# Padding tiles move the large SBUF tiles of a two-layer backbone to multiples of 512 bytes

## The chip, the cores and the metric

The kernel runs on one core of a Trainium2 chip. The metric is the device time of one execution in microseconds (us), as the median of several runs. The engines are named as the profile names them: PE is TensorE's stream of matmuls and PEld its weight loads, DVE is VectorE, ACT ScalarE, POOL GpSimd, and SP the queue from which most transfers are issued. A matmul multiplies a stationary operand, which a weight load brings into the array first, with a moving operand, whose columns then stream through.

## The reference

The reference is a two-layer diffusion backbone on 1024 latent tokens with 256 context tokens in front of them, 1024 features wide, in float32.

```
for i in range(DEPTH):                       # DEPTH = 2
    sh1, sc1, g1, sh2, sc2, g2 = modulation(c, w_mod[i], b_mod[i])
    h = x * (1.0 + sc1) + sh1
    if i % 2 == 0:  y = retention_gla_mixer(h, ...) @ ev_w_out[j]     # 4 retention + 4 gated heads
    else:           y = window_attention(q, k, v, k_c, v_c, sink) @ od_w_out[j]
    x = sublayer_residual(x, y, g1, ln_g[i, 0], ln_b[i, 0])           # LayerNorm(alpha * x + gate * y)
    x = sublayer_residual(x, sq_relu_mlp(x * (1.0 + sc2) + sh2, mlp_w1[i], mlp_w2[i]), g2, ...)
```

The context tokens go through layer 0 as well and serve layer 1 as keys and values. The MLP is 4096 wide with a squared ReLU.

## The kernel before

All 1280 tokens are kept with features on partitions, in three chunks of 256, 512 and 512 tokens. Each float32 operand of a large product is split into two parts, `hi` and `lo` (tiles in float32r), and each product is three matmuls: hi x hi, hi x lo, lo x hi (`mm3`, L196 to L199). Weights come in by units of 128x1024: `wsplit` (L180 to L187) loads `raw`, ScalarE copies it to the `hi` half of a tile `w`, and GpSimd (or VectorE) subtracts for the `lo` half. Each tile `w` has 8 KB in every partition.

The stages in order of time are: the modulation vectors and layer 0's projections (`first_proj`, `unit_loop`, to about 180 us); the values and the reverse pass (L483 to L602, to 360 us), where the activations `xh`, `xl` are the stationary operand and the weights `wvh`, `wvl` move (L540 to L542); the forward pass with gates, output projection and residual (to 725 us); layer 0's MLP (`mlp`, L956, to 1730 us); layer 1's queries, keys and values (L1171 to L1226, to 1900 us), where again the activations `hh`, `hl` are stationary and the weights `w` move (L1201 to L1203); windowed attention with its output projection (to about 2420 us); layer 1's MLP. In the MLPs and projections of L197 to L199 the weights `w` are stationary and the activations (`hh`, `hl`, `uh`, `ul`, `yh`, `yl`) move, with 512 or 256 columns.

No planner sets the order: it is the order in which the code issues work, and each engine runs its own queue with waits on semaphores. What the change touches is memory alone. The pools are stacked in SBUF from both ends of a partition: a pool with `side="right"` grows down from the upper end, the others grow up from the lower end. `cp` (L47), the first pool on the left, holds small constants; above it lie the raw weights and the activations. On the right lie the weight tiles `w` (`w_b1`, L219, later `wg`, L483), layer 0's residual stream `acc` (`acp0`, L697) and then the keys (`kvp`, L1172). The built program gives these starts within a partition, in bytes modulo 512:

| tiles | before | after |
|---|---|---|
| weights `w` (all stages), `acc` of layer 0 | 480 | 0 |
| activations `hh`, `hl`, `uh`, `ul`, `yh`, `yl`, `xh`, `xl` | 448 | 0 |
| weights `wvh`, `wvl` of the values' stage | 448 | 0 |
| landing buffers of the weights (`rawp`) | 448 | 0 |
| first modulation weights and x in `b1` (`raw` of L230, `xs`), `lwh`, `lwl` | 0 | 64 |
| keys `kall` | 32 | 64 |
| `cs`, `ident` | 192 | 256 |

Of the kernel before, what the change touches and what calls it, by code (L numbers as in the profile page):

```python
# [19 lines left out]
P = 128  # L20
# [14 lines left out]
def backbone(ctx: ExitStack, tc: tile.TileContext, xT, cin, wmod, bmod, lng, lnb, w1, w2,  # L35
# [10 lines left out]

    cp = ctx.enter_context(pool(name="cp", bufs=1))  # L47
    rawp = ctx.enter_context(pool(name="rawp", bufs=3))
    es_p = ExitStack()
# [8 lines left out]
    def ring(*ids):  # L58
        """PSUM banks taken in turn."""
        state = [0]  # L60

        def take():
            i = ids[state[0] % len(ids)]
            state[0] += 1
            return psum.tile([P, 512], F32, tag=f"k{i}", name=nm(f"k{i}"), bufs=1)
        return take

    pM = ring(7)

# [1 line left out]
    def const(shape, name, dt=F32, pool_=None):  # L71
# [21 lines left out]

# [1 line left out]
    mod = const([2, 6, 8, 2], "mod")  # L95
# [3 lines left out]
    def mod_steps(l, s, mdp, nb=1, w=1024, tags=("raw",), bank=None):  # L99
        """Generator: one weight load and its products per step; the vectors at the end."""  # L100
        pM_ = bank or pM
# [31 lines left out]
    def mod_chunks(l, s, bank):  # L133
        """As mod_steps, 512 outputs at a time; yields the index of the chunk that a step belongs to."""
        for q in range(4):
            pt = bank()
            for k in range(0, KT, 2):
                raw = rawp.tile([P, 1024], F32, tag="raw", name=nm("raw"))
                SY.dma_start(raw.rearrange("p (a c) -> p a c", a=2),
                             wmod[l, k * P:(k + 2) * P, s * 2048 + q * 512:s * 2048 + q * 512 + 512]  # L140
                             .rearrange("(a p) c -> p a c", p=P))
                yield q
                for a in range(2):
                    for g in range(4):
                        TE.matmul(pt[32 * g:32 * g + 32, 0:P], lhsT=cs[:, k + a, :],
                                  rhs=raw[:, a * 512 + g * P:a * 512 + g * P + P], start=(k + a == 0),
                                  stop=(k + a == KT - 1))
            mt = cp.tile([P, P], F32, tag="mt", name=nm("mt"))
            S.copy(mt, pt[:, 0:P])
            TE.transpose(pt[:, P:2 * P], mt, ident)  # L150
            idx = 2 * s + q // 2
            ks = slice(4 * (q % 2), 4 * (q % 2) + 4)
            V.tensor_tensor(mod[:, l, idx, ks, :], pt[:, P:2 * P].rearrange("p (g i) -> p g i", g=4)[:, :, 0:2],
                            bm[:, l, idx, ks, None].to_broadcast([P, 4, 2]), ALU.add)
            if idx in (1, 4):
                V.tensor_scalar(osc[:, l, idx // 3, ks], mod[:, l, idx, ks], 1.0, None, op0=ALU.add)
            if idx in (2, 5):
                V.tensor_scalar(gta[:, l, idx // 3, ks], mod[:, l, idx, ks], 1.0 / ALPHA, None, op0=ALU.mult)
            yield q
# [13 lines left out]
    def reserve(pool, tags):  # L173
        """Fix the order of a pool's tags in memory."""
        for tag, shape, dt, nb in tags:
            for _ in range(nb):
                pool.tile([P] + shape, dt, tag=tag, name=nm(tag), bufs=nb)

# [1 line left out]
    def wsplit(pool, src, eng=None):  # L180
# [26 lines left out]

# [1 line left out]
    def dram(name, shape):  # L209
# [14 lines left out]
    def first_load(q):  # L224
        """Weights of the shifts and scales of feature tiles 2 q, 2 q + 1; two tiles of the sum per buffer."""
        raws = []
# [30 lines left out]
    SY.dma_start(bm, bmod.rearrange("p (l s k) -> p l s k", l=2, s=6))  # L257
# [1 line left out]
    th = const([16], "th")  # L259
# [39 lines left out]

    # ================= layer 0: projections (feature-major) =================  # L300
    def make_h(src, l, idx, j, hh, hl, tp, tag, nb=1, hi_eng=None):
# [3 lines left out]
    def h_steps(src, l, idx, j, hh, hl, tp, tag, nb=1, hi_eng=None, los=(V, G)):  # L305
        """h = src * (1 + scale) + shift, as an exact (hi, lo) pair; all (P, 8, n)."""
        n = src.shape[2]
# [11 lines left out]
    with es_b1:  # L319
# [37 lines left out]

        # lgm columns: 0-7 (d, h) on all rows; 8-11 (d, pair) in pair rows; 12-15 h in (f|b) rows
        S.activation(dret, lgm[:, 12:16], AF.Exp, scale=128.0)
# [9 lines left out]

        # low-rank gates  # L370
        gk = b1.tile([32, 4, P], F32, tag="gk", name="gk")
# [109 lines left out]

    # ================= values and reverse pass =================
    wg = ctx.enter_context(pool(name="wg", bufs=5, side="right"))  # L483
# [126 lines left out]
    def layer_norm_steps(acc, l, s, tp, ts, tq, nb, pe_sums, pL, qn=1024, tail=None):  # L610
        """acc (P, 8, n) <- LayerNorm over the features, in place."""
        n = acc.shape[2]
# [3 lines left out]
        def part(pp, src, g0, g1):  # L616
            """column groups g0..g1 of pp: sums over features of tiles 2 g, 2 g + 1 of src."""
            for kk in range(2):
# [4 lines left out]
        def mean(pp, i):  # L623
            """PSUM tile with the mean over all features on every partition."""
            pm = pL()
# [54 lines left out]
    def w_out_steps(y, wsrc, wp, acc, l, j, pW, engs=(None, None), wnext=None):  # L680
        """acc (P, 8, n) += gate / alpha * (y @ W)"""
        n = acc.shape[2]
# [10 lines left out]

    # ================= forward pass, output projection, first residual =================
    accs, hs = {}, {}
# [12 lines left out]
    with pool(name="b3", bufs=1) as b3:  # L708
# [6 lines left out]
        def load_acc(ci, o0, after):  # L715
            """A part of the residual stream, once a tile has been written."""
            G.tensor_copy(accs[ci][:, 0, o0:o0 + 1], after)
# [31 lines left out]
        def gproj(p_, g_, ln):  # L749
            """silu of the gate projections of a pair of tiles"""  # L750
            ci = chunk_of(2 * p_)
# [56 lines left out]
        for tp_ in range(NT // 2):  # L808
# [20 lines left out]
            for t in (2 * tp_, 2 * tp_ + 1):  # L829
# [30 lines left out]
                Sprev = St  # L860
                # scores (s on partitions)
                Pr = b3.tile([P, 4, P], F32, tag="Pr", name=nm("Pr"), bufs=1)
# [91 lines left out]

    # ================= MLP =================
    def mlp(l, chunks, hs, accs, wp, mp, post, fill=iter(()), tick=lambda k: None, ticks=None, early=None):  # L956
# [74 lines left out]
    class Early:  # L1031
        """Work for the first block of an MLP, in two streams that are advanced between its steps."""

# [17 lines left out]
    def new_h(hp, ci, l, mp, os_=(0, 256), los=(V, G)):  # L1051
        """Streams' parts for h of a chunk."""
        if ci not in hs:
# [51 lines left out]

    # ================= layer 1: queries, keys, values =================
    qTd = [[dr.tile([2, 2, 64, 4, P], F32, tag=f"qT{n}_{i}", name=f"qT{n}_{i}") for i in range(2)] for n in range(8)]
# [25 lines left out]
    def rotate(dst, src, nh, n):  # L1133
        """dst = src rotated; head layout (u1 32 | u2 32); src in PSUM."""
        rp = p1.tile([P, 2, 64], F32, tag="rp", name=nm("rp"), bufs=2)
# [9 lines left out]
    def transposed(kr, nj, name):  # L1145
        """kr (P, 128 nj) -> (P, 2, nj, 128): its blocks transposed, as an exact (hi, lo) pair."""
        pk = pE()
# [19 lines left out]
    for grp in range(3):  # L1167
        wu = []
        if grp == 1:
            es_a.close()  # L1170
            kvp = ctx.enter_context(ExitStack())  # L1171
            kp = kvp.enter_context(pool(name="kvp", bufs=1, side="right"))  # L1172
            kall = kp.tile([P, 2, 4, T], F32R, tag="kall", name="kall")
            wmask = const([2, P], "wmask", BF16, kp)
# [55 lines left out]

    # ================= layer 1: windowed attention, output projection, residual =================
    acp = ctx.enter_context(pool(name="acp1", bufs=1))
    hy = ctx.enter_context(pool(name="hy", bufs=1))
    yall = [hy.tile([P, KT, 512], F32R, tag=f"y{i}", name=f"y{i}") for i in "hl"]
    with pool(name="p2", bufs=1) as p2:
# [31 lines left out]
        def group(n, g):  # L1267
            """Steps of one block of queries and one group of heads: scores of four heads, then the keys' tiles."""
            blks = [b_ for b_ in (n - 1, n, n + 1) if 0 <= b_ < 8]
# [119 lines left out]

    # ================= layer 1: MLP, output =================  # L1390
    kvp.close()
# [27 lines left out]

# [1 line left out]
def _fm(w):  # L1421
    """(1024, 128 u) -> (u, 128, 8 * 128): per unit of 128 output columns."""
    u = w.shape[1] // P
# [3 lines left out]
def _col(v):  # L1427
    """(..., 1024) -> (128, ... * 8), features on partitions."""
    v = v.reshape(-1, KT, P)
# [3 lines left out]
def layout(x, c, ctx, c_ctx, w_mod, b_mod, ln_g, ln_b, mlp_w1, mlp_w2, ev_w_in, ev_ret_theta, ev_gla_gk_w,  # L1433
# [3 lines left out]
    d = {}  # L1437
# [29 lines left out]
    wqkv = od_w_qkv[0]  # L1467
    # head columns in the order (pair member, axis, frequency)
    wr = wqkv[:, :1280].reshape(1024, 20, 2, 2, 16).transpose(0, 1, 3, 2, 4).reshape(1024, 1280)
# [4 lines left out]
    d["wo1"] = _fm(od_w_out[0])  # L1474
    # constants of the shapes
    s = np.arange(P)[:, None]
# [43 lines left out]
```

## Time and profile before

| | us |
|---|---|
| median of 3 runs | 3056.57 |
| lowest and highest run | 3055.7, 3057.76 |
| span of the profiled execution | 3055.1 |

The profiled execution's own time is not listed beside the runs; its span, from the first instruction to the last, is 1.5 us shorter than the median.

A row of the page or of the trace gives the engine, the operation, output and inputs by the program's names with the shape, how often it occurs, its busy time and the mean duration. Durations of matmuls are modelled at their end, and consecutive ones overlap in the record: a matmul of 512 columns is recorded with about 0.40 us while the next one starts 0.23 us after it. What one costs in a dense stream is therefore read from starts, in the timeline.

### The profile page before, as it was taken

The page shows a single profiled execution, that of the slowest core. Times are in us where ns is not written, and L with a number is a line of the kernel's source. Part 1 is how long each engine was busy: PE and PEld are TensorE (multiplying, and loading weights), DVE is VectorE, ACT ScalarE, POOL GpSimd, SP SyncE. Part 2 cuts the span into 40 slices and gives each one's busy share as a digit, 9 for nine tenths or more (in the row PEclk, how much of TensorE's full clock was granted, in tenths as well). Part 3 has the DMA queues.
Part 4 walks back from the last instruction along what each step waited for, and adds up shares of the span by engine and source line. Part 5 has one row for each costly group of instructions (what it writes and reads, how often), then busy time and mean ns, then how long its engine had stood idle before and what let it go on. Part 6 is the DMA issues. An engine that isn't in the chain of part 4 may idle for free. (4 is left out here: it accounts for less than half of the span.)

```text
span 3055.1 us, 43318 instructions
## 1 busy us (share of the span) xinstructions
PE 2950.5 (97%) x17856; PEld 2376.8 (78%) x17856; DVE 1520.5 (50%) x2489; ACT 975.6 (32%) x1617; POOL 811.2 (27%) x609
## 2 busy tenths in 40 slices
PE   7989998999999999999999999999999999999997
PEld 4766788888878787778888777677678888888886
DVE  3654478777433333333334554666775333433336
ACT  4433344444211111111111532556653112112113
POOL 3120145544211111111110432244343122122111
PEclk9999999999999999999999999999999999999999
DMA  7367685663222222221100276122221111111011
GB/s 251 102 224 241 184 262 193 200 200 114 80 73 70 69 80 69 73 69 45 42 32 11 75 205 185 50 79 87 63 90 43 48 56 49 35 56 55 30 40 56
DMA packets 164261, 304.52 MB, mean 100 GB/s; under 512 B 13504, under 2 KB 90560, under 8 KB 163552
## 3 DMA queue, kind: packets, MB, share of 16 engines
q1 hardware_dynamic: 145648, 272.91, 28.0%
q0 software_dynamic: 6480, 16.26, 2.0%
q10 hardware_dynamic: 11936, 12.59, 1.5%
q8 instruction: 140, 2.29, 0.3%
q14 instruction: 57, 0.47, 0.0%
HBM read 257.67 MB, written 44.04 MB: 99 GB/s over the span
## 5 line engine op out<-in xcount | busy, mean ns | idle before, releaser
L186 POOL TENSOR_TENSOR w<-raw,w 128x1024 fp32r<-128x1024 f32 x210 | 508.3, 2428 | 1711.8 <-ACT w L185 1671.0
L996 DVE SCALAR_TENSOR_TENSOR acc<-k,gta,acc 128x512 f32<-128x512 f32 (+1 forms) x704 | 444.3, 649 | 861.9 <-PE k L199 855.2
L197 PE MATMUL k<-hh,w 128*128 128x256 f32 (+1 forms) x1632 | 559.5, 343 | 5.2 <-DVE hh L193 3.4
L198 PE MATMUL k<-hl,w 128*128 128x256 f32 (+1 forms) x1632 | 558.0, 342 | 4.1 <-POOL hl L194 3.5
L199 PE MATMUL k<-hh,w 128*128 128x256 f32 (+1 forms) x1632 | 554.0, 340 | 0.2 <-POOL w L186 0.2
L185 ACT CAST w<-raw 128x1024 fp32r<-128x1024 f32 x260 | 269.1, 1046 | 839.8 <-PE k L199 544.6
L197 PE MATMUL k<-uh,w 128*128 128x512 f32 (+1 forms) x1408 | 506.5, 360 | 4.0 <-DVE acc L996 3.9
L198 PE MATMUL k<-ul,w 128*128 128x512 f32 (+1 forms) x1408 | 499.6, 355 | 0.0
L199 PE MATMUL k<-uh,w 128*128 128x512 f32 (+1 forms) x1408 | 498.7, 354 | 0.0
L197 PEld LDWEIGHTS k<-hh,w 128*128 128x128 f32 x1632 | 309.7, 190 | 59.4 <-issue 16.3
L198 PEld LDWEIGHTS k<-hl,w 128*128 128x128 f32 x1632 | 309.8, 190 | 49.7 <-issue 7.4
L199 PEld LDWEIGHTS k<-hh,w 128*128 128x128 f32 x1632 | 310.0, 190 | 39.0 <-issue 2.8
L197 PEld LDWEIGHTS k<-uh,w 128*128 128x128 f32 x1408 | 264.7, 188 | 60.5 <-issue 13.6
L978 ACT ACTIVATE r<-k 128x512 f32<-128x512 f32 (+1 forms) x176 | 91.0, 517 | 665.7 <-PE k L199 664.8
L199 PEld LDWEIGHTS k<-uh,w 128*128 128x128 f32 x1408 | 264.9, 188 | 41.8 <-issue 1.0
L198 PEld LDWEIGHTS k<-ul,w 128*128 128x128 f32 x1408 | 264.8, 188 | 40.4 <-issue 0.8
L197 PE MATMUL k<-yh,w 128*128 128x256 f32 (+1 forms) x544 | 184.3, 339 | 10.3 <-DVE acc L690 10.3
L198 PE MATMUL k<-yl,w 128*128 128x256 f32 (+1 forms) x544 | 181.5, 334 | 0.0
L199 PE MATMUL k<-yh,w 128*128 128x256 f32 (+1 forms) x544 | 181.1, 333 | 0.0
L981 DVE TENSOR_TENSOR r<-r 128x1024 f32<-128x1024 f32 (+1 forms) x88 | 114.1, 1297 | 125.6 <-ACT uh L980 125.4
L670 POOL TENSOR_SCALAR acc<-acc,lg_t,lb_t 128x256 f32<-128x256 f32 x124 | 103.3, 845 | 115.6 <-DVE acc L664 46.6
L1306 DVE TENSOR_REDUCE sm<-pS 128x1 f32<-128x640 f32 (+1 forms) x128 | 100.9, 788 | 46.4 <-PE pS L1304 44.6
(300 smaller groups left out, 4415.7 us busy)
## 6 DMA issues: line engine op xcount, KB each, us to landing
raw<-in_w SPq DMA_DIRECT2D x128, 512.0 KB, 3.4
raw<-in_wo SPq DMA_DIRECT2D x72, 512.0 KB, 3.5
raw<-in_wmod SPq DMA_DIRECT2D x128, 256.0 KB, 2.7
raw<-in_wfm SPq DMA_DIRECT2D x48, 512.0 KB, 5.7
raw<-in_wmod SPq DMA_DIRECT2D x32, 512.0 KB, 4.3
kt<-kd SPq DMA_DIRECT2D x20, 512.0 KB, 5.6
qt<-qT POOLq DMA_DIRECT2D x32, 256.0 KB, 4.3
qT<-qT ACTq DMA_DIRECT2D x30, 256.0 KB, 3.7
```

Of the source, the lines that this page charges most:

```text
L185: S.copy(hi, raw)
L186: (eng or G).tensor_tensor(lo, raw, hi.bitcast(F32), ALU.subtract)
L197: TE.matmul(pt, lhsT=wh, rhs=xh, start=start, stop=False)
L198: TE.matmul(pt, lhsT=wh, rhs=xl, start=False, stop=False)
L199: TE.matmul(pt, lhsT=wl, rhs=xh, start=False, stop=stop)
L670: G.tensor_scalar(acc[:, k, :], acc[:, k, :], lg_t[:, l, s, k:k + 1], lb_t[:, l, s, k:k + 1], op0=ALU.mult, op1=ALU.add)
L978: S.activation(rf[:, i, :n], pts[i][:, :n], AF.Relu)
L981: V.tensor_tensor(rf[:, :, :n], rf[:, :, :n], rf[:, :, :n], ALU.mult)
L996: V.scalar_tensor_tensor(a_, pt[:, :n], gta[:, l, 1, m, cj(ci):cj(ci) + 1], a_, op0=ALU.mult, op1=ALU.add)
L1306: V.tensor_reduce(sm_[:, 0, i:i + 1], sall, AX.X, ALU.max)
```

## The change

Three tiles are allocated that no instruction writes or reads: 64 bytes in each partition at the beginning of `cp`, 480 bytes at the upper end of SBUF in a new pool `edge`, and 64 bytes at the beginning of `kvp`. Comments and docstrings go as well; they aren't shown.

```
     cp = ctx.enter_context(pool(name="cp", bufs=1))
+    cp.tile([P, 16], F32, tag="pad", name="pad")
+    edge = ctx.enter_context(pool(name="edge", bufs=1, side="right"))
+    edge.tile([P, 120], F32, tag="edge", name="edge")
     rawp = ctx.enter_context(pool(name="rawp", bufs=3))
...
             kp = kvp.enter_context(pool(name="kvp", bufs=1, side="right"))
+            kp.tile([P, 16], F32, tag="pad", name="kpad")
             kall = kp.tile([P, 2, 4, T], F32R, tag="kall", name="kall")
```

On PE, DVE, ACT and SP the built programs hold the same instructions with the same waits in the same order. On POOL one wait moves. It stands at the beginning of the forward pass, where `load_acc` (L715 to L718) writes one column of an `acc` tile before that tile is loaded: left and right stacks come to lie 544 bytes nearer to each other, and so a part of `acc` that had to wait for the end of an older transfer is another one. On POOL, before:

```order
L786 COPY dcm<-g_2854 128x1 [waits Activation_49]
L717 COPY acc_371_2831<-g_2854 128x1 [waits DMAHW2_49,DMAHW7_49,DMAHW0_49,Pool_49]
L836 COPY S_3190<-g_2854 128x1
L845 COPY kt_3198<-g_2854 128x1
L186 TENSOR_TENSOR w_3007<-raw_3005,w_3007 128x1024 [waits PE_49,Activation_49]
L763 TENSOR_SCALAR g_2854<-g_2854,ng 128x256 [waits DMASW1_49,DMASW0_49,Activation_49]
L717 COPY acc_371_2831<-g_2854 128x1 [waits Pool_49]
```

On POOL at the same place, after the change (three lines have been added above, so L717 is L720, and the buffers' numbers are higher by five):

```order
L789 COPY dcm<-g_2859 128x1 [waits Activation_49]
L720 COPY acc_371_2836<-g_2859 128x1 [waits DMAHW7_49,DMAHW0_49,Pool_49]
L839 COPY S_3195<-g_2859 128x1
L848 COPY kt_3203<-g_2859 128x1
L189 TENSOR_TENSOR w_3012<-raw_3010,w_3012 128x1024 [waits PE_49,Activation_49]
L766 TENSOR_SCALAR g_2859<-g_2859,ng 128x256 [waits DMASW1_49,DMAHW2_49,DMASW0_49,Activation_49]
L720 COPY acc_371_2836<-g_2859 128x1 [waits Pool_49]
```

The wait for the transfers' semaphore DMAHW2 has gone from the copy into `acc` to the scaling of `g` four instructions later (and, with its higher count, to the copy into the next `acc` tile).

## Rows read from the trace of the kernel before

**Rows 1.** The page, busy time, share of the span and instructions of each engine.

```profile
PE 2950.5 (97%) x17856; PEld 2376.8 (78%) x17856; DVE 1520.5 (50%) x2489; ACT 975.6 (32%) x1617; POOL 811.2 (27%) x609
```

**Rows 2.** Busy us by stage, then granted clock, transfer engines' share, GB/s.

```profile
360.00:725.00 365.00, 332.88 (x2802) 304.81 (x2803) 269.12 (x414) 165.58 (x235) 173.41 (x110) 0.97 0.64 207
725.00:1730.00 1005.00, 998.42 (x6063) 820.75 (x6062) 407.51 (x598) 203.16 (x304) 197.18 (x107) 1.00 0.20 62
2420.00:3055.00 635.00, 619.71 (x2912) 502.36 (x2910) 257.81 (x333) 130.10 (x177) 129.44 (x65) 0.99 0.14 46
```

**Rows 3.** Timeline of PE in layer 0's MLP: start us, duration us, instruction.

```profile
1391.16 0.40 PE L198 MATMUL k<-hl,w 128*128 128x512 f32 x1
...
1393.96 0.40 PE L198 MATMUL k<-hl,w 128*128 128x512 f32 x1
```

**Rows 4.** Timeline at half clock, values' stage; then that stretch: us, busy, clock.

```profile
197.37 0.63 PE L540 MATMUL k<-wvh,xh 128*128 128x512 f32 x1
...
199.07 0.61 PE L541 MATMUL k<-wvl,xh 128*128 128x512 f32 x1
...
197.40:199.00 1.60, 1.60 (x5) 0.50 1.10 290
```

**Rows 5.** Timeline of PE in layer 1's projections, twelve starts later.

```profile
1754.09 0.40 PE L1202 MATMUL pS<-w,hh 128*128 128x512 f32 x1
...
1756.89 0.40 PE L1202 MATMUL pS<-w,hh 128*128 128x512 f32 x1
```

**Rows 6.** Timeline of PE in the values' stage, ten and then twelve starts later.

```profile
344.80 0.39 PE L542 MATMUL k<-wvh,xl 128*128 128x512 f32 x1
...
347.10 0.39 PE L540 MATMUL k<-wvh,xh 128*128 128x512 f32 x1
...
349.82 0.39 PE L540 MATMUL k<-wvh,xh 128*128 128x512 f32 x1
```

**Rows 7.** Groups by line and shape: count, busy us, mean ns, idle before.

```profile
L197 PE MATMUL k<-uh,w 128*128 128x512 f32 x896 | 358.1, 400 | 0.0
L197 PE MATMUL k<-hh,w 128*128 128x512 f32 x800 | 319.0, 399 | 0.0
L197 PE MATMUL k<-yh,w 128*128 128x512 f32 x224 | 88.6, 395 | 0.0
L1201 PE MATMUL pS<-w,hh 128*128 128x512 f32 x144 | 58.8, 408 | 0.0
L1201 PE MATMUL pO<-w,hh 128*128 128x512 f32 x64 | 25.9, 405 | 0.0
L197 PE MATMUL k<-hh,w 128*128 128x256 f32 x832 | 240.5, 290 | 5.2 <-DVE hh L193 3.4 <-ACT g L761 1.8
L197 PE MATMUL k<-uh,w 128*128 128x256 f32 x512 | 148.4, 290 | 4.0 <-DVE acc L996 3.9
L197 PE MATMUL k<-yh,w 128*128 128x256 f32 x320 | 95.7, 299 | 10.3 <-DVE acc L690 10.3
```

**Rows 8.** Timeline of PE, 128x256 matmuls before the first MLP, twelve starts later.

```profile
718.83 0.28 PE L197 MATMUL k<-yq,w 128*128 128x256 f32 x1
...
720.25 0.28 PE L197 MATMUL k<-yq,w 128*128 128x256 f32 x1
```

**Rows 9.** The first 60 us as in rows 2; waits on transfers: us, times, longest.

```profile
0.00:60.00 60.00, 45.73 (x384) 23.39 (x384) 23.07 (x58) 24.86 (x37) 15.44 (x15) 1.00 0.81 282
...
PE k L239 <- DMA raw<-in_wmod: 7.8, 5, 6.0
...
PEld k L239 <- DMA raw<-in_wmod: 5.0, 7, 1.5
```

**Rows 10.** Groups by line and shape on POOL: the `lo` halves of the weights.

```profile
L186 POOL TENSOR_TENSOR w<-raw,w 128x1024 fp32r<-128x1024 f32 x210 | 508.3, 2428 | 1711.8 <-ACT w L185 1671.0 <-issue 40.1 <-POOL w L186 0.7
L502 POOL TENSOR_TENSOR wvl<-raw,wvh 128x1024 fp32r<-128x1024 f32 x5 | 13.2, 2668 | 18.5 <-ACT wvh L501 18.5
```

More of the change, by code (lines that the diff above doesn't have):

```diff
@@ L47, in backbone @@
     cp = ctx.enter_context(pool(name="cp", bufs=1))
+    cp.tile([P, 16], F32, tag="pad", name="pad")
+    edge = ctx.enter_context(pool(name="edge", bufs=1, side="right"))
+    edge.tile([P, 120], F32, tag="edge", name="edge")
     rawp = ctx.enter_context(pool(name="rawp", bufs=3))
@@ L1172, in backbone @@
             kp = kvp.enter_context(pool(name="kvp", bufs=1, side="right"))
+            kp.tile([P, 16], F32, tag="pad", name="kpad")
             kall = kp.tile([P, 2, 4, T], F32R, tag="kall", name="kall")
```

## The prediction

> **What bounds the kernel now.** I read four views, in this order. The page's first line comes first: TensorE (PE) is busy for 2950.5 us of a span of 3055.1 us, every other engine for half of it or less [rows 1]. The table by stage says where that share is a true bound: in the first layer's MLP (725 to 1730 us) PE is busy 998.42 us of 1005, in the last one (2420 to 3055 us) 619.71 of 635, while VectorE, the next engine, has 407.51 us of the 1005 [rows 2]. There a change in PE's pace goes straight into the time. A busy PE need not be at its peak, though, because the end of a matmul is modelled. So the third view is the timeline, and there I read only starts: the distance from one start to the next is what a matmul really takes out of the stream.
>
> In the MLP twelve 128x512 matmuls start between 1391.16 and 1393.96 us: 2.80 / 12 = 233.3 ns each [rows 3]. At half the clock (1.2 GHz, the granted clock of 0.50 in that row) four such matmuls start between 197.37 and 199.07 us, 425 ns each [rows 4]; half of that is about 213 ns, which is 512 columns at 2.4 GHz. So at full clock a matmul takes some 20 ns longer than its columns, and at half clock it does not. Something that doesn't scale with TensorE's clock costs 20 ns of 233.
>
> The fourth step is the comparison on which the forecast rests. Two stages have the same shape of work: an activation tile is the stationary operand and is used for two of three matmuls, a weight tile of 512 columns moves. In layer 1's projections (L1201 to L1203) the weights start at 480 modulo 512 in their partition and the activations at 448; the matmuls start 2.80 us apart per twelve, 233.3 ns [rows 5]. In the values' stage of layer 0 (L540 to L542) weights and activations both start at 448; from 347.10 to 349.82 us twelve matmuls take 2.72 us, 226.7 ns [rows 6]. The MLP, with the 448 and 480 in the other roles, is at 233.3 again. So 6.7 ns of the 20 go with the placement: 448 against 448 is fast, 448 against 480 slow, whichever of the two moves. The difference of the two starts is 32 bytes, half of 64.
>
> **The change part by part.** No instruction is added, removed or put in another order: three tiles that nobody writes or reads move all others. The left stack of SBUF moves by 64 bytes (448 becomes 0 modulo 512), the right one by 480 bytes down (480 becomes 0), the keys' pool by another 64. After it, all weight and activation tiles of the large matmuls start at 0, so their starts differ by a multiple of 64, as in L540's stage.
>
> (1) 128x512 matmuls against split weights. The groups hold 896, 800 and 224 per line for L197 to L199, and 144 + 64 per line for L1201 to L1203 [rows 7]: 3 x 1920 + 3 x 208 = 6384. If each goes from 233.3 to 226.7 ns, that is 6384 x 6.67 = 42.6 us. From this comes a start-up loss: L540's stage is not at 226.7 from its first matmul. From 344.80 to 347.10 us ten of them take 2.30 us, 230 ns, before the fast pace sets in [rows 6]: 33 ns lost at each new start. With a break every 24 to 96 matmuls, which is what the timeline of the MLPs shows, I take 200 breaks: 200 x 33 ns = 7 us. The part comes to 42.6 - 7 = 36 us. Its bounds are 0 (the placement is not the cause) and 6384 x 20 = 128 us (all of the excess goes).
>
> (2) 128x256 matmuls. The three large groups have 832, 512 and 320 per line, 4992 together [rows 7]; twelve of them start within 1.42 us, 118.3 ns each, 11.6 ns above half of 213.3 [rows 8]. No row has this shape with equal starts, so the gain is bounded: 0 at one end; at the other the same two thirds of the excess that L540's stage keeps, a gain of 3.9 ns, 4992 x 3.9 = 19 us. I take 10 us, the middle, since many of these lie in the gated stage, 360 to 725 us, where PE is busy for 332.88 us of 365 [rows 2] and part of a gain goes into waits.
>
> (3) The transfers at the start. Here the change works the other way: the buffers of the first modulation weights and of x (`raw` in `b1`, `xs`) start at 0 modulo 512 now and at 64 after it. In the first 60 us the transfer engines are busy for 0.81 and move 282 GB/s, 348 GB/s per full share; in 360 to 725 us, where most landing buffers start at 448, it is 207 / 0.64 = 323 GB/s [rows 2, 9]. If the whole 7% came from the start of the buffer, 60 x 0.81 x 0.07 = 3.4 us of transfers would be added, and PE does wait for them: 7.8 us before matmuls and 5.0 us before weight loads of L239 [rows 9]. I take 0, the mix of sizes explains as much, and keep 3.4 us as the bound on the slow side.
>
> (4) Work on the other engines. GpSimd's subtraction takes 2428 ns into tiles at 480 and 2668 ns, in five cases, into tiles at 448 [rows 10]: nothing there favours a start, and GpSimd, ScalarE and VectorE wait for PE in the MLPs. 0 us; a gain there would be hidden behind PE. One wait of GpSimd on a transfer goes from an L717 copy to later ones: the transfer was over at the earlier place, so it costs 0, and behind it stand only copies that need it anyway.
>
> Sum: 36 + 10 = 46 us. The profiled span is 3055.1 us, 1.5 us under the median of 3056.57; I take the median as the execution's time and get 3056.6 - 46 = 3011 us (-1.5%).
>
> One page speaks against all this. The Trainium skill, in "SBUF — State Buffer", Specifications (TRN2), gives SBUF lines of 16 bytes, with a penalty for each step to a new line. By that rule alone 448, 480 and 0 are equally good, because each is a multiple of 16, the sum would be 0 and the time 3057 us. Rows 5 and 6 differ by 6.7 ns although both keep to the rule, so the trace doesn't bear it out as the whole story.
>
> **The rivals.** (A) *The offset isn't the cause.* L540's stage also differs from L1201's in where its tiles lie (its weights are in the middle of the partition, those of L1201 at the upper end) and in what the other engines do meanwhile. Against this speaks that the MLPs keep 233.3 ns with quite different neighbours, and that L1201 is the same pattern of operands. Time: 3057 us, or 3060 us with the transfers of (3) on top; both count as no change here, since about 0.2% (6 us) is what a measurement of this kernel can tell from none.
>
> (B) *More than the step to 226.7 ns.* If a start at a full multiple of 512 takes the whole excess away, as at half clock, (1) gives 6384 x 20 = 128 us and (2) 4992 x 11.6 = 58 us: 3057 - 186 = 2871 us. For it: the excess isn't tied to the columns [rows 4]. Against it: no stage before has a moving operand at 0, so nothing shows it.
>
> The Trainium skill, in "TensorE: Matmul & The Clock Gate", Back-to-back issue gap, gives N / 2.4 + 2.5 ns, that is 215.8 ns for 512 columns. An estimate by that page would be 6384 x 17.5 = 112 us for (1); rows 3 and 6 are both above it.
>
> (C) *Equal starts collide.* The readers of the MLP (PE's two operands, VectorE, ScalarE, GpSimd) would all begin at the same place modulo 512, where 480 and 448 are now staggered. If the 6.7 ns have the other sign for 0 against 0, a 128x512 matmul takes 240 ns and the time is 3057 + 42 = 3099 us. It decides in the MLPs, from the point where equal starts cost more than the stagger. Against it: L540's stage has equal starts and is the fastest there is.
>
> **How the numbers follow.** Forecast 0.58, A 0.26, B 0.10, C 0.06. The forecast's own range comes from the bounds: 3057 - 42.6 - 19 = 2995 us without start-up loss and with the full (2), 3057 - 36 + 3.4 = 3024 us without (2) and with the transfers. The range of 8 in 10 takes the forecast and A: 2985 to 3062 us, which leaves out B and C. Faster by over 0.2%: forecast and B, 0.68; within 0.2%: A, 0.26; slower: C, 0.06.
>
> **What would show it.** In the changed kernel's timeline the MLP's 128x512 matmuls should start 226.7 ns apart, and L1201's too; L540's should stay at 226.7 (B: below it, all of them). The 128x256 ones should lie between 114.4 and 118.3 ns. The number of instructions on each engine should be the same, and PE's waits on `raw` at L239 should not exceed the present ones by more than 3.4 us. I am wrong if the starts in the MLP stay 233.3 ns apart, and wrong in size if they fall below 226.

## The result and the profile after

The changed kernel takes 3026.18 us (median of 4 runs, 3017.06 to 3031.19) against 3057.16 us for the kernel before (median of 4 runs, one more than in the table above, 3055.7 to 3062.05). The ratio is 0.9895 with a 95% interval of 0.9876 to 0.9915: 31 us less, where 46 were forecast. The profiled execution took 3027.12 us with a span of 3025.3 us, 29.8 us below the span before.

The page's first line after the change answers to [rows 1]: busy time, share of the span and number of instructions for each engine.

```profile
PE 2922.6 (97%) x17856; PEld 2386.6 (79%) x17856; DVE 1525.4 (50%) x2489; ACT 976.4 (32%) x1617; POOL 809.9 (27%) x609
```

The counts are the same and PE is still busy for 97%. PE's busy time falls by 27.9 us; no other engine's falls by more than 1.3 us, and that of the weight loads rises by 9.8 us. So PE itself became faster, as the forecast said, and the place to look is again the distance from one start to the next.

The timeline of PE after the change (start us, duration us, instruction): layer 0's MLP with 512 columns, twenty-four starts apart; then layer 1's projections and the values' stage, twelve apart.

```profile
1243.52 0.39 PE L201 MATMUL k<-hl,w 128*128 128x512 f32 x1
...
1248.96 0.39 PE L201 MATMUL k<-hl,w 128*128 128x512 f32 x1
1741.19 0.39 PE L1206 MATMUL pS<-w,hh 128*128 128x512 f32 x1
...
1743.91 0.39 PE L1206 MATMUL pS<-w,hh 128*128 128x512 f32 x1
316.91 0.39 PE L543 MATMUL k<-wvh,xh 128*128 128x512 f32 x1
...
319.63 0.39 PE L543 MATMUL k<-wvh,xh 128*128 128x512 f32 x1
```

5.44 us / 24 = 226.7 ns where [rows 3] had 233.3; 2.72 / 12 = 226.7 ns in the projections where [rows 5] had 233.3; and the same 226.7 ns as before in the values' stage [rows 6]. For 512 columns that is the forecast to the digit. The 256-column matmuls are the surprise. The same 24 of them in layer 0's MLP, in the timeline of before and then of after:

```profile
1441.40 0.28 PE L197 MATMUL k<-uh,w 128*128 128x256 f32 x1
...
1444.24 0.28 PE L197 MATMUL k<-uh,w 128*128 128x256 f32 x1
```

```profile
1429.65 0.28 PE L200 MATMUL k<-uh,w 128*128 128x256 f32 x1
...
1432.53 0.28 PE L200 MATMUL k<-uh,w 128*128 128x256 f32 x1
```

2.84 / 24 = 118.3 ns before, as in [rows 8], and 2.88 / 24 = 120.0 ns after: these became slower. The starts of all matmuls of the two traces, put into groups, give the account. A step counts as regular between 215 and 250 ns for 512 columns and between 105 and 135 ns for 256; the others are breaks, waits and half clock. The total is the time of all steps of a group.

```
                              regular steps, mean ns        total of all steps, us
                              before         after          before    after    change
512 columns, w stationary     5613  233.32   5613  227.13   1368.6   1333.4    -35.2
512 columns, w moving          578  233.12    578  228.69    153.2    152.6     -0.6
512 columns, wvh or wvl        411  228.36    424  228.19    125.7    121.5     -4.2
256 columns, w stationary     5485  118.31   5445  119.64    784.9    794.3     +9.4
```

Together -30.6 us, and the span moved by -29.8. So the 512-column matmuls with `w` gave the 36 us that were forecast, and the 256-column ones took a quarter of it back. The 4.2 us on `wvh` and `wvl` are no change of pace: their regular step is the same within 0.2 ns, and 13 fewer of them are irregular.

### The profile page after: what moved, and what is told of

Same layout as the page of the kernel before. It is cut to its first block, busy times and chain, and to the rows that moved or that the text cites. A ratio compares the mean times of both kernels' runs of the same rounds, so it can differ in the third digit from the quotient of the medians.

```text
span 3025.3 us, 43318 instructions
## 1 busy us (share of the span) xinstructions
PE 2922.6 (97%) x17856; PEld 2386.6 (79%) x17856; DVE 1525.4 (50%) x2489; ACT 976.4 (32%) x1617; POOL 809.9 (27%) x609
## 5 line engine op out<-in xcount | busy, mean ns | idle before, releaser
L189 POOL TENSOR_TENSOR w<-raw,w 128x1024 fp32r<-128x1024 f32 x210 | 507.4, 2424 | 1683.4 <-ACT w L188 1642.9
L200 PEld LDWEIGHTS k<-uh,w 128*128 128x128 f32 x1408 | 266.5, 189 | 55.4 <-issue 14.2
L200 PEld LDWEIGHTS k<-yh,w 128*128 128x128 f32 x544 | 106.5, 196 | 22.6 <-DVE acc L693 11.5
```

Source lines behind the costliest of these rows:

```text
L189: (eng or G).tensor_tensor(lo, raw, hi.bitcast(F32), ALU.subtract)
L200: TE.matmul(pt, lhsT=wh, rhs=xh, start=start, stop=False)
```

## The experiments

**Two tiles and nothing else.** The first run measures the disputed cost by itself. It leaves the whole model out and runs matmuls from one `mov` and one `sta` tile, both beginning at a multiple of 512; the starts within them are set for every series.

```
+    for mo, so, n in SERIES:        # starts in bytes, columns; 48 matmuls each
+        series(mo, so, n)
...                                  # in series, for every k:
+                m, s = mo // 4 + k * n, so // 4 + k * P
+                xh, xl = mov[:, m:m + n], mov[:, m + 4096:m + 4096 + n]
+                wh, wl = sta[:, s:s + P], sta[:, s + 1024:s + 1024 + P]
+                TE.matmul(pt, lhsT=wh, rhs=xh, start=(k == 0), stop=False)
...                                  # then wh with xl, wl with xh
```

> This kernel leaves the whole model out: PE alone runs 66 series of 48 float32r matmuls in the order hi x hi, hi x lo, lo x hi, with 512 or 256 columns, from two tiles whose starts are varied in steps of 32 bytes (and 4, 8, 16, 48). Theory 1, the difference of the two starts modulo 64 decides: 512 columns step at 226.7 ns wherever the difference is a multiple of 64 and at 233.3 ns where it is 32 more, 256 columns at 120.0 and 118.3 ns, both for all absolute starts. Theory 2, the multiple of 512 decides: 226.7 ns only at 0 against 0, 233.3 ns everywhere else. Theory 3, the starts are not the cause: one step for all series of one width.

Its timeline of PE, twenty-four starts apart, for four series in order of time: 512 columns with the moving tile at 0 and the stationary one at 0, then 32 and 0, 256 columns with 0 and 0, 512 columns with 448 and 448:

```profile
77.23 0.39 PE L73 MATMUL k<-mov,sta 128*128 128x512 f32 x1
...
82.67 0.39 PE L73 MATMUL k<-mov,sta 128*128 128x512 f32 x1
...
99.14 0.40 PE L73 MATMUL k<-mov,sta 128*128 128x512 f32 x1
...
104.74 0.40 PE L73 MATMUL k<-mov,sta 128*128 128x512 f32 x1
...
263.87 0.28 PE L73 MATMUL k<-mov,sta 128*128 128x256 f32 x1
...
266.75 0.28 PE L73 MATMUL k<-mov,sta 128*128 128x256 f32 x1
...
407.78 0.39 PE L73 MATMUL k<-mov,sta 128*128 128x512 f32 x1
...
413.22 0.39 PE L73 MATMUL k<-mov,sta 128*128 128x512 f32 x1
```

That is 5.44 / 24 = 226.7 ns, 233.3, 120.0 and again 226.7 ns. Read in this way for every series (the mean of the last 24 steps, ns, the stationary tile at 0):

```
start of the moving tile   0      32     64     96     128    160    192    224
512 columns                226.7  233.3  228.9  233.3  233.3  234.2  233.3  233.3
256 columns                120.0  117.8  117.8  120.0  118.5  118.8  117.8  118.3
start of the moving tile   256    288    320    352    384    416    448    480
512 columns                226.7  233.3  228.9  233.3  233.3  234.2  233.3  233.3
256 columns                120.0  117.8  117.8  120.0  118.5  118.8  117.8  118.3
```

Theory 3 falls: with nothing else running and only the starts changed, the steps of the kernel come back. Theory 2 falls: 256 against 0, 448 against 448 and 480 against 480 (not in the table) are as fast as 0 against 0. For 512 columns theory 1 holds in its core, that the difference of the two starts decides, but not in its period. The row repeats after 256 bytes, not 64; a difference of 64 gives 228.9, and of 128 or 192 gives 233.3. And 512 columns are fastest at equal starts, where 256 columns are slowest of their row, as they are at 96. For 256 columns the difference alone is not enough: with the stationary tile moved up, 0 against 64 took 113.3 ns, although 192 against 0 has the same difference modulo 256 and took 117.8, and 0 against 480 took 116.7 ns in one series and 117.8 in another.

**The kernel with one pad.** Two kernels take the change apart. In the first only `w` and `acc` move, to 448, where the activations have always been:

```
+    edge = ctx.enter_context(pool(name="edge", bufs=1, side="right"))
+    edge.tile([P, 8], F32, tag="edge", name="edge")
```

> One pad of 32 bytes at the upper end and none else: w and acc move from 480 to 448, the activations stay at 448, nothing starts at a multiple of 512. Theory 1 (difference modulo 64): the 512-column matmuls of L197 to L199 step at 226.7 ns, the 256-column ones at 120.0, and the time is that of the changed kernel, 3026 us (3015 to 3035). Theory 2 (multiples of 512): 233.3 and 118.3 ns, 3057 us. Theory 3 (not the starts, but something else that the pads bring): 3057 us.

It takes 3021.16 us, a ratio of 0.9891 (0.9861 to 0.9922) to the kernel before, the changed kernel's gain with neither the weights nor the activations of the large matmuls at a multiple of 512. Its timeline, at the places shown above:

```profile
1244.84 0.39 PE L200 MATMUL k<-hl,w 128*128 128x512 f32 x1
...
1250.28 0.39 PE L200 MATMUL k<-hl,w 128*128 128x512 f32 x1
1430.36 0.28 PE L199 MATMUL k<-uh,w 128*128 128x256 f32 x1
...
1433.24 0.28 PE L199 MATMUL k<-uh,w 128*128 128x256 f32 x1
```

5.44 / 24 = 226.7 and 2.88 / 24 = 120.0 ns, both as in the changed kernel. What the change does is make two starts equal. The second kernel has the lower pad alone: the activations at 0, `w` at 480.

```
     cp = ctx.enter_context(pool(name="cp", bufs=1))
+    cp.tile([P, 16], F32, tag="padl", name="padl")
```

> The pad of 64 bytes at the lower end alone: the activations move from 448 to 0, w stays at 480. Theory 1: the difference stays 32 modulo 64, the steps stay 233.3 and 118.3 ns in L197 to L199, 3057 us (3050 to 3062). Theory 2, as far as it is the moving tile's multiple of 512 that counts: 226.7 ns in L197 to L199 and 3026 us.

It takes 3050.82 us, a ratio of 0.9993 (0.9983 to 1.0004): no change, although every activation now starts at a multiple of 512.

```profile
1244.54 0.39 PE L199 MATMUL k<-hl,w 128*128 128x512 f32 x1
...
1250.14 0.39 PE L199 MATMUL k<-hl,w 128*128 128x512 f32 x1
1433.27 0.28 PE L198 MATMUL k<-uh,w 128*128 128x256 f32 x1
...
1436.07 0.28 PE L198 MATMUL k<-uh,w 128*128 128x256 f32 x1
```

The 512-column step stays at 5.60 / 24 = 233.3 ns, as theory 1 said. The 256-column step does not stay at 118.3 but goes to 2.80 / 24 = 116.7 (mean of 5465 regular ones 117.0): the sign of the difference, +32 in place of -32, counts too. By the steps alone that is some 7 us. The medians show 2 us of it, and the interval allows 5 at most.

**The upper pad alone** puts `w` at 0 and leaves the activations at 448.

```
+    edge = ctx.enter_context(pool(name="edge", bufs=1, side="right"))
+    edge.tile([P, 120], F32, tag="edge", name="edge")
```

> The pad of 480 bytes at the upper end alone: w starts at 0, the activations stay at 448, a difference of -64. Theory 1 as it was first put (modulo 64): 226.7 and 120.0 ns in L197 to L199, 3026 us. Theory 1 modulo 256: 512 columns stay at 233.3 ns, 256 columns go from 118.3 to between 113.3 and 117.8 ns, 5485 x 0.5 to 5.0 ns = 3 to 27 us, so 3026 to 3052 us. Theory 2 (a multiple of 512 for the weights, as the change is named for them): 226.7 ns.

Measured: 3043.57 us, ratio 0.9956 (0.9935 to 0.9977). This run tells the two periods apart inside the kernel, by its timeline in the MLP and in the projections (L1204, where `w` moves, so that the difference is +64 there):

```profile
1250.01 0.39 PE L200 MATMUL k<-hl,w 128*128 128x512 f32 x1
...
1255.61 0.39 PE L200 MATMUL k<-hl,w 128*128 128x512 f32 x1
1438.29 0.28 PE L199 MATMUL k<-uh,w 128*128 128x256 f32 x1
...
1441.02 0.28 PE L199 MATMUL k<-uh,w 128*128 128x256 f32 x1
1748.67 0.39 PE L1204 MATMUL pS<-w,hh 128*128 128x512 f32 x1
...
1751.41 0.39 PE L1204 MATMUL pS<-w,hh 128*128 128x512 f32 x1
```

512 columns keep 5.60 / 24 = 233.3 ns at -64 and go to 2.74 / 12 = 228 ns at +64: the two entries of the table, and not the 226.7 that a period of 64 would give. So theory 1 as the prediction put it is wrong for 512 columns, and the mended one right. The 256-column matmuls are at 2.73 / 24 = 113.8 ns (mean of 5423 regular ones 114.9). From 118.3 to 114.9 is 18.7 us, and the time shows 11. The profiled execution is the slowest of the five, 3051.91 us. In it the total of these matmuls falls by 7.9 us only (784.9 to 777.0), because 529 steps are irregular in place of 467; its mean granted clock is 0.982, against 0.987 before. If the clock is either full or half, that is 0.018 x 2 x 3050 = 110 us at half clock in place of 79, and so some 15 us of work lost; this is an estimate from the rounded clocks. The other four executions have clocks of 0.984 to 0.986; the three with 0.986 took 3039.88 to 3043.57 us, and the one of the kernel before on the same chip with 0.986 took 3059.24. At equal clocks the gain is thus 16 to 19 us, which is that of the steps. Over all runs the clock lay between 0.982 and 0.986 here and between 0.984 and 0.988 before; whether the faster stream brings the half-clock stretches on or they fell there by chance, these runs don't tell.

**Where do the 13 ns that are left come from?** The 512 columns alone would take some 213 ns, half of what they take at half clock [rows 4]. The next run leads every series in with 24 matmuls of 512 columns at equal starts. It repeats the differences, moves the low half of the moving operand by itself (`lo`), and makes the stationary tile narrower (`mc`).

```
-                xh, xl = mov[:, m:m + n], mov[:, m + 4096:m + 4096 + n]
-                wh, wl = sta[:, s:s + P], sta[:, s + 1024:s + 1024 + P]
+                xh, xl = mov[:, m:m + n], mov[:, m + lo // 4 + 4096:m + lo // 4 + 4096 + n]
+                wh, wl = sta[:, s:s + mc], sta[:, s + 1024:s + 1024 + mc]   # mc 128, 64 or 32
...
+        series(0, 0, 0, 512, P, 1)       # after every series
```

> The model is left out again. Series of 96 matmuls, each led in by 24 of 512 columns with equal starts, so that every series begins from the same state. Theory 1 as bench_starts has mended it: the difference moving minus stationary counts modulo 256, 512 columns take 226.7 ns at 0, 228.9 at 64, 233.3 to 234.2 elsewhere; 256 columns take 120.0 ns at 0 and 96, 116.7 to 118.8 elsewhere, and a stationary start 64 above the moving one may give 113.3 (seen in one series of 48). Rival: 113.3 came from what ran before, then it is 117.8 here. Why a step is longer than its columns: if the weight load, which runs beside the matmul before, takes reading slots from the moving operand, a stationary tile of 64 or 32 columns instead of 128 brings the excess of 512 columns from 13.3 to about 6.7 and 3.3 ns; if the excess belongs to the matmul itself, it stays 13.3.

For 512 columns the mended theory holds: all seven differences, now made by moving the stationary tile, come within 1.3 ns of the table. For 256 columns it holds in part. From the same lead-in it makes no difference which of the two tiles is moved, within 0.5 ns, except at 160 (118.6 and 117.3 ns). A difference of 192, this time as 0 against 64, gives 117.75 to 117.79 ns in all four parts of its series, so the 113.3 of the run before depended on what ran ahead of it. But 128 gives 120.0 ns, where the run before had 118.5 and 116.7 to 118.8 had been expected: what runs ahead counts there too.

Nor does each matmul's own difference add up to the step. With equal starts but for the low half of the moving operand, 32 bytes further, two of three matmuls have a difference of 0 and one of 32, which by the table would average 228.9 ns:

```profile
618.24 0.39 PE L74 MATMUL k<-mov,sta 128*128 128x512 f32 x1
...
623.80 0.39 PE L74 MATMUL k<-mov,sta 128*128 128x512 f32 x1
```

It is 5.56 / 24 = 231.7 ns, and with 64 in place of 32 it is 231.3 to 232.7 where 227.4 would follow; 128 and 192 do give the 228.9 of the average. So a matmul's own two starts are not all that counts, and equal starts gave 512 columns the full 226.7 ns only when both halves of the moving operand had them, as in the changed kernel.

The question of the weight load got an answer that neither side had expected. The timeline of two series with 64 stationary columns and equal starts, 512 and then 256 moving columns:

```profile
801.00 0.40 PE L74 MATMUL k<-mov,sta 128*64 128x512 f32 x1
...
806.52 0.40 PE L74 MATMUL k<-mov,sta 128*64 128x512 f32 x1
...
906.10 0.28 PE L74 MATMUL k<-mov,sta 128*64 128x256 f32 x1
...
908.82 0.28 PE L74 MATMUL k<-mov,sta 128*64 128x256 f32 x1
```

512 columns take 5.52 / 24 = 230.0 ns, longer than the 226.7 with 128 stationary columns, and 231.7 with 32 of them. 256 columns take 2.72 / 24 = 113.3 ns, shorter than 120.0, but 117.8 with 32. So the excess doesn't shrink with the size of the weight load, and that explanation is dropped. It isn't a fixed property of the matmul either, since it changes with the stationary tile's width. What remains is what both runs show: the step depends on how the starts of the moving and of the stationary operand lie to each other. The cause behind that, and with it the 13 ns, stays open.

**A version for both shapes.** If equal starts suit 512 columns and a difference of -64 suits 256, each can have its own. This kernel is `w_at_448` with the operands of 4032 of the 5952 256-column matmuls 192 bytes further on, which is 64 below `w` modulo 256.

```
     hg = es_hg.enter_context(pool(name="hg", bufs=1))
+    hg.tile([P, 48], F32, tag="hgpad", name="hgpad")          # ahead of hh0, hl0
...                                                            # and in the same way ahead of yh, yl
...
     uh = mp.tile([P, 2, 512], F32R, tag="uh", name=nm("uh"), bufs=2)
+    if n == 256:
+        uh, r = uh[:, :, 48:304], r[:, :, 48:304]
```

> Built on w_at_448: the 512-column matmuls keep equal starts, and where a 256-column operand has a tile of its own or room in its tile (hh0, hl0, yh, yl, and uh, ul with 256 columns), it is put 192 bytes further, 64 below w modulo 256: 4032 of the 5952 256-column matmuls. Theory 1 modulo 256: 512 columns at 226.7 ns as in the changed kernel, the 4032 at about 115.0 instead of 119.7 ns as in right_pad_only, 4032 x 4.7 ns = 19 us less than the changed kernel, about 3005 us. If the gain of right_pad_only does not hold where 256 columns follow 512 columns with equal starts (the series of bench_pairs that were led in so kept 117.8), 4032 x 1.9 ns = 8 us, about 3015 us.

> The changed kernel as it is, timed on the same chip as both_shapes: 0.9895 of the kernel before, 3023 to 3027 us by all theories.

It takes 3018.35 us, a ratio of 0.987 (0.9855 to 0.9886) to the kernel before, against 3023.05 us and 0.9889 (0.9872 to 0.9906) for the changed kernel on the same chip. That is the lowest median of all kernels here, but the two intervals overlap, and it is above both times that had been expected (3005 and 3015 us). The timeline shows the steps, 512 and 256 columns, at the usual places:

```profile
1234.47 0.39 PE L200 MATMUL k<-hl,w 128*128 128x512 f32 x1
...
1239.91 0.39 PE L200 MATMUL k<-hl,w 128*128 128x512 f32 x1
1419.29 0.28 PE L199 MATMUL k<-uh,w 128*128 128x256 f32 x1
...
1422.11 0.28 PE L199 MATMUL k<-uh,w 128*128 128x256 f32 x1
```

226.7 ns and, here, 2.82 / 24 = 117.5. Over the whole trace the moved 256-column matmuls have regular steps of 114.8 to 115.7 ns on average, a mixture of the two paces of 113.3 and 117.8 that the series showed for the same starts, and the others 118.9 to 120.0. All 256-column matmuls on `w` together take 781.3 us, against 792.9 in the execution of the changed kernel that was profiled beside it: 11.6 us less, of the 19 expected. The span is only 2.8 us shorter (3016.2 against 3019.0 us). Where the rest went is seen when the two traces are cut at the same instructions: at the 1501st matmul, at the first of layer 1's projections, and at the 12001st, where the output projection of layer 1 has begun. This kernel, and then the changed one, with PE, weight loads, VectorE, ScalarE and GpSimd in the columns of [rows 2]:

```profile
0.00:293.10 293.10, 261.88 (x1501) 187.22 (x1502) 150.34 (x270) 121.25 (x184) 56.27 (x33) 0.96 0.64 207
293.10:1700.90 1407.80, 1364.90 (x9194) 1166.06 (x9192) 704.32 (x1081) 386.48 (x574) 371.60 (x220) 0.99 0.33 105
1700.90:1964.50 263.60, 250.23 (x1312) 185.70 (x1309) 137.82 (x266) 114.13 (x239) 81.91 (x103) 0.97 0.49 137
```

```profile
0.00:288.80 288.80, 258.51 (x1500) 185.62 (x1501) 151.42 (x270) 121.38 (x185) 55.89 (x33) 0.97 0.65 210
288.80:1710.80 1422.00, 1384.47 (x9193) 1183.83 (x9191) 707.22 (x1081) 386.68 (x573) 370.19 (x220) 0.99 0.33 104
1710.80:1968.70 257.90, 247.98 (x1313) 183.73 (x1310) 140.07 (x266) 114.23 (x239) 81.69 (x103) 0.98 0.49 140
```

In the long middle stretch, where most of the moved matmuls lie, the kernel is 14.2 us faster. It loses 4.3 us ahead of it, where no moved operand is used yet, 5.7 us behind it, in the projections (where all 512-column matmuls but 48 of 624 keep their starts) and the beginning of the attention, and 1.4 us in the remainder. The granted clock is lower by 0.01 in both of the shorter stretches, some 3 us in each; the remainder of the loss is not explained. Executions of one and the same program differ as much: the first 1500 matmuls took 294.3 us in the first profiled execution of the changed kernel and 288.8 us in the second. So the gain of the steps is shown, and that of the whole kernel, beyond the changed one, is not.

## Why the prediction was right, and where it was not

**What bounds the kernel** held: PE's pace in the dense stages went straight into the time.

**The range** holds, 3026.18 us in 2985 to 3062, but not by the forecast's own terms: these allowed 3024 us at most, and the range reaches further only because rival A was let into it.

**(1) 512 columns: right, in mechanism and size.** 5613 x (233.32 - 227.13) ns = 34.7 us and 578 x (233.12 - 228.69) ns = 2.6 us make 37.3 us, where 36 were forecast. The start-up loss was put at 7 us; by the mean over the steady 226.67 it is 5613 x 0.46 + 578 x 2.02 ns = 3.8 us.

**The reason given for it was half right.** "Their starts differ by a multiple of 64" is not the condition: right_pad_only has a difference of -64 and stays at 233.3 ns. Equal starts modulo 256 are. The prediction came out because the change makes the starts equal, which satisfies both; that it did not need to tell the two apart was luck. The comparison of L540's stage with L1201's, on which it rested, was sound: it was a difference of 0 against one of 32. Its argument from half clock set equal starts [rows 4] beside unequal ones at full clock [rows 3]. The trace of before has the missing rows, with a difference of -32 at a granted clock of 0.50:

```profile
715.15 0.41 PE L198 MATMUL k<-yq,w 128*128 128x256 f32 x1
...
716.43 0.41 PE L198 MATMUL k<-yq,w 128*128 128x256 f32 x1
```

Six steps take 1.28 us, 213.3 ns each, about half of the 425 ns of 512 columns in [rows 4]. So at half clock the step goes with the columns alone, at unequal starts too.

**(2) 256 columns: the step that failed.** The gain was bounded by 0 and 19 us and put at 10 us, by carrying "the same two thirds of the excess" from 512 columns to 256. It is a loss: 5445 x (119.64 - 118.31) ns = 7.2 us, 9.4 us with the irregular steps. (The forecast's 4992 matmuls left out those with `yq` and with other outputs; there are 5952.) The shape had no row with equal starts, and the bound should have gone below nothing, since no reason excluded a loss. The 17 us between +10 and -7 are the difference between the forecast of -46 and the measured -31 us, but for 2 us.

**(3) The transfers at the start** were put at 0, with 3.4 us as the bound, and no cost shows in the time. In the first 60 us after the change, the same view as [rows 9]:

```profile
0.00:60.00 60.00, 45.65 (x384) 23.39 (x384) 22.77 (x58) 24.62 (x37) 14.79 (x15) 1.00 0.82 282
```

```profile
PE k L242 <- DMA raw<-in_wmod: 8.4, 3, 6.0
...
PEld k L242 <- DMA raw<-in_wmod: 5.8, 7, 2.0
```

The rate is 282 GB/s as before and the share 0.82 for 0.81, so 344 GB/s per full share for 348: 1%, and not the 7% of the bound. The waits of matmuls and weight loads are 14.2 us for 12.8, 1.4 us more.

**(4) The other engines**: GpSimd's subtraction takes 2424 ns for 2428 [rows 10], as forecast. The wait that moved on GpSimd shows nowhere: at the beginning of the forward pass its waits are the same within 0.1 us.

```profile
L189 POOL TENSOR_TENSOR w<-raw,w 128x1024 fp32r<-128x1024 f32 x210 | 507.4, 2424 | 1683.4 <-ACT w L188 1642.9 <-issue 39.8 <-POOL w L189 0.6
```

**The rivals.** A falls with bench_starts, where the starts are the only thing that changes: 0, 32 and 64 against 0 take 226.7, 233.3 and 228.9 ns. The Trainium skill's "SBUF — State Buffer", Specifications (TRN2), gives lines of 16 bytes with a penalty for each step to a new one, and by that alone these three would be equally good, which the trace doesn't bear out. B falls because 0 against 0 is no better than 448 against 448. The Trainium skill's "TensorE: Matmul & The Clock Gate", Back-to-back issue gap, has a formula for the isolated gap that gives 215.8 ns for 512 columns; the lowest steady step of this width that any run here shows is 226.7. C, equal starts cost more, is wrong for 512 columns and has the right sign for 256: it was on the list, but for the wrong shape. Its reason, engines that collide, is not shown, and other engines aren't needed for it, since PE runs alone in bench_starts.

## What to carry to other kernels

When every matmul of a dense stream takes longer than its columns, compare the starts of the moving and the stationary tile in their partition before the tiles' alignment: here the difference of the two, modulo 256 bytes, set the step of 512 columns, and no tile had to begin at a multiple of 512. Try the difference for each width of matmul apart, because the best one for 512 columns was among the slowest for 256, and in the kernel itself, because with 256 columns what ran ahead moved the step by up to 4 ns. Compare executions at equal granted clock where the effect is a few us. And give a term whose shape no row shows bounds of both signs.

## What was not expected of the hardware

- For float32r with 128 stationary columns the steady step of 512 columns was 226.7 ns at equal starts, 228.9 at a difference of +64 and 232.1 to 234.4 at the other multiples of 32. The row repeats every 256 bytes. Of 256 columns, led in by 512 columns at equal starts, it was 120.0 ns at differences of 0, +96 and +128, and 116.5 to 118.7 at the others.
- At half clock the placement costs nothing: 213.3 ns for 256 columns at a difference of -32.
- Smaller offsets matter as well: with the moving tile 4, 8 and 16 bytes above the stationary one, 512 columns took 238.0, 233.3 and 231.7 ns.
- The same starts can give two paces, kept for a whole series: 256 columns at a difference of -64 ran at 113.3 ns in one series and at 117.8 in another, and in the kernels at a mixture of 115.
- A matmul's own two starts are not all: with the low half of the moving operand 32 bytes off, one matmul in three, 512 columns took 231.7 ns on average, where the steps of the three differences average 228.9.
- A narrower weight load doesn't make the step shorter in a simple way: with 64 stationary columns at equal starts 512 columns took 230.0 ns and 256 took 113.3.
